# Three pairs of k-tiles by seven products instead of two in both output products of a streaming-encoder block

## The chip, the core and the metric

The kernel runs on one core of a Trainium2 chip. The metric is the device time of one execution in microseconds (us). TensorE (PE in the profile, with its weight loads as PEld), VectorE (DVE), ScalarE (ACT), GpSimd (POOL) and SyncE (SP, which issues the loads and stores here) each work through a queue of their own, in order, and wait for each other by semaphores.

## What is computed

One layer of an encoder block on 256 frames of width 2048, in float32. The residual stream `x` passes four parts, and the two whose last product changes stand in the middle:

```python
x = x + 0.5 * swiglu(rms_norm(x, ffn1_norm), ffn1_w_gate, ffn1_w_up, ffn1_w_down)
proj = rms_norm(x, mix_norm) @ w_in             # 2048 x 4112
x = x + concat([y_pool, y_gla]) @ w_out         # mixer's output product, 2048 x 2048
q = rms_norm(x, xattn_norm) @ w_q               # attention over 256 memory tokens
x = x + o @ w_o                                 # attention's output product, 2048 x 2048
x = x + 0.5 * swiglu(rms_norm(x, ffn2_norm), ffn2_w_gate, ffn2_w_up, ffn2_w_down)
return rms_norm(x, final_norm)
```

`y_pool` and `y_gla` (the pooling and the gated linear attention of the mixer) and `o` (four heads of 512) lie as the left operand `ys`; the activations of the other products lie as `xs`.

## The kernel before

**Precision.** TensorE multiplies in a reduced format (fp32r). Each operand is therefore split into a high part (a cast on ScalarE) and a remainder (a subtraction on VectorE), and each product is three on TensorE: high by high, high by remainder, remainder by high. The parts of a weight tile are called `wh` and `wl`, made at L1572 and L453.

**Units.** All weights are streamed. A unit is one load of 1 MB from `in_w...` into `raw` (L627, three buffers), the making of its parts, and its products. `Stream.emit` (L70) writes the making of unit u+2 in front of the products of unit u (`AHEAD` = 2), and a load three units ahead. From there a scheduler sets the order on each engine; `in_turn` and `among_weights` keep the makings, and what is put among them, in a fixed order on VectorE and ScalarE.

**The output products.** `into_x` (L821) runs two blocks of 1024 output columns. A block is eight units, one for each pair of k-tiles (256 rows of the weights), in the order that `orders` gives. A plain unit (L556) has 2 column halves x 2 row halves x 2 k-tiles x 3 = 24 products of 128x128 by 128x512 (L362). A unit whose pair is in `sevens` (L539) takes the 2x2x2 block product in a Strassen-Winograd form: 7 block products instead of 8, so 21 products (L507). It needs other operands: of the weights four sums `T` (three additions on VectorE, L486) and their parts (`wh` by L489, `wl` by L453) beside the parts of the three other weight blocks (`xh` by L279, `xl` by L280); of the activations sums that `Sums.make` (L413) forms once for each pair (L424 to L436, the splits at L285 and L286) and keeps in the tile `ye` and in `ys` itself. `OUTPUT` (L816) holds the pairs, the orders and the sums of both output products; `make_sums` (L810) says behind how many units each pair's sums are written.

**Joining and hand-over.** The partial sums of the sevens have four banks of their own. Behind the last seven of a block, `combine` (L570) joins them (L574 to L579) and `early_parts` (L765) adds them into `x` (L770). At the end of the block, two additions (L758) add the rest, `store_x` (L750) stores `x`, and `fold` (L785) turns it: 16 transposes (L791), eight splits on ScalarE (L248) and on VectorE (L240), and the squares for the norm (L800). Behind block 2 comes `finish_norm` (L299, L212 to L224). The next stage reads the folded `xs`: the attention's queries behind the mixer (L1366), the second feed-forward behind the attention.

**Homes.** In these stages `T`, `xh` and `xl` have no tiles of their own; `OUT_HOMES` (L1227) gives them in turn the tiles `kv`, `att` and `PT` of the attention.

Of the kernel before, what the change touches and what calls it, by code (L numbers as in the profile page):

```python
# [99 lines left out]
def build(ctx, tc, I, out):  # L100
# [90 lines left out]
    ys = main.tile([P, KT, 2, S], F32R, tag="ys", name="ys")  # L191
# [212 lines left out]
    class Sums:  # L404
# [4 lines left out]
        def __init__(self, name, act, pairs, over, room):  # L409
            self.name, self.act, self.pairs, self.over = name, act, pairs, over  # L410
            self.room, self.where = room, {}
# [390 lines left out]
    class IntoX:  # L802

        def __init__(self, pairs, after, orders, sevens, over=True):
            self.sums = Sums("ye", ys, pairs, over, 2)
            self.after, self.orders, self.sevens = after, orders, sevens

        def make_sums(self, after=None):  # L810
            for g, n in zip(self.sums.pairs, after or self.after):
# [1 line left out]

    WHOLE = IntoX((0, 4), (2, 5), ((1, 2, 3, 5, 0, 6, 4, 7), (1, 2, 0, 3, 4, 5, 6, 7)),
                  ((0, 4), (0, 4)))
    OUTPUT = IntoX((0, 4), (0, 4), ((1, 2, 3, 5, 0, 6, 4, 7), (1, 2, 0, 3, 4, 5, 6, 7)),  # L816
                   ((0, 4), (0, 4)))
    REST = IntoX((0,), (2,), ((1, 2, 3, 4, 0, 5), None), ((0,), ()), False)
    END = IntoX((0,), None, None, None)

    def into_x(w, act, scale, gain=None, k0=0, nk=KT, spread_too=True, src=None, way=OUTPUT):  # L821

        for b in range(2):
            st.op(lambda b=b: fetch_x(b, src), 2)
            cols = wwide(w, b * 2 * NB, k0, nk)
            if way.sevens[b]:
                block_s(cols, act, way.sums, way.orders[b], residual(scale, b, 0),
                        early_parts(scale, b), way.sevens[b])
            else:
                block_t(cols, act, residual(scale, b))  # L830
            if gain is not None:
                for j in range(2):
                    st.op(lambda c=2 * b + j: fold(c, gain), 1)
        if gain is not None:
            st.op(lambda: finish_norm(4, spread_too), 2)
            if spread_too:
                st.op(spread_norm, 3)
# [395 lines left out]
    def homes(of):  # L1233
        return lambda: scope.update(shared={tag: list(of[tag]) for tag in of})
# [35 lines left out]
                )  # L1270
        split_four(xs, 4 * c, v, G_MEM)

    OUTPUT.make_sums((1, 4))
    into_x(I["w_out"][0], ys, 1.0, G_X, spread_too=False)
    st.op(homes(Q_HOMES))
    st.op(mem_in, 2)
# [111 lines left out]
    st.op(homes(OUT_HOMES))  # L1388
    OUTPUT.make_sums()
    into_x(w_o, ys, 1.0, G_FFN2, spread_too=False)  # L1390
# [201 lines left out]
def program(shapes):  # L1592
    import concourse.bacc as _bacc

    nc = _bacc.Bacc("TRN2", target_bir_lowering=False, num_devices=1)
    args = {
        name: nc.dram_tensor(f"in_{name}", shapes[name], F32, kind="ExternalInput").ap()
        for name in _INS
    }
    out = nc.dram_tensor("out", _OUT, F32, kind="ExternalOutput").ap()  # L1600
    with tile.TileContext(nc, schedule_with_timeline_sim=True) as tc, ExitStack() as ctx:
        build(ctx, tc, args, out)
    return nc
# [10 lines left out]
```

## Time and profile before

| | |
|---|---|
| median of 3 runs | 2083.93 us (2083.45 to 2084.53) |
| profiled execution | 2082.87 us, span 2081.1 us, mean granted clock 0.999 |
| TensorE busy | 2069.4 us, 9660 recorded products |
| VectorE, ScalarE, GpSimd busy | 1786.8, 1138.7, 98.4 us |
| HBM read, written | 417.58 MB, 16.78 MB |

The page gives busy time by engine and then the chain of work that ended last, followed back from the last instruction. The costliest groups name the line, the engine, the tile written and the tiles read: `wl<-T,wh` at L453 is the remainder of a seven's sums, `wl<-raw,wh` the remainder of a plain tile. A timeline lists instructions by start and duration; a row with x2 holds two. Windows give the busy time of each engine between two times. All times count from the span's start.

### The profile page before, as it was taken

How to read it: one execution, taken by the hardware profiler on the slowest of the kernel's cores; microseconds unless marked ns; L12 is line 12 of the kernel's file. 1: busy time of each engine (PE TensorE's matmuls, PEld its weight loads, DVE VectorE, ACT ScalarE, POOL GpSimd, SP SyncE). 2: the span in 40 equal slices, each digit the busy share in tenths (PEclk: the TensorE clock that was granted, in tenths of full speed). 3: DMA queues.
4: the chain of work that ended last, by engine and by line, in shares of the span. 5: the costliest groups of instructions: out<-in, count | busy, mean ns of one | idle time of the engine just before them, and what ended most of it. 6: DMA issues, size and time to landing. Idle time of an engine off the chain costs nothing.

```text
span 2081.1 us, 24346 instructions
## 1 busy us (share of the span) xinstructions
PE 2069.4 (99%) x9660; PEld 1727.4 (83%) x9660; DVE 1786.8 (86%) x1670; ACT 1138.7 (55%) x1128; POOL 98.4 (5%) x87
## 2 busy tenths in 40 slices
PE   9999999999999999999999999999999999999998
PEld 7888888888888888888888888888888888888886
DVE  7998899989998677679788777879988999889987
ACT  7655455644654545455755444656554555545554
POOL 0000000000000000000000000000100010000001
PEclk9999999999999999999999999999999999999999
DMA  7666666566656755557655455666576665676664
GB/s 264 208 199 228 234 223 220 184 222 240 225 200 218 249 166 182 162 185 272 227 179 189 161 182 181 204 222 204 181 243 215 234 209 191 224 242 222 211 226 150
DMA packets 131322, 435.95 MB, mean 209 GB/s; under 512 B 9860, under 2 KB 13544, under 8 KB 130824
## 3 DMA queue, kind: packets, MB, share of 16 engines
q1 hardware_dynamic: 131176, 434.38, 61.8%
q8 instruction: 76, 1.25, 0.2%
q14 instruction: 38, 0.31, 0.0%
q10 hardware_dynamic: 32, 0.01, 0.0%
HBM read 417.58 MB, written 16.78 MB: 209 GB/s over the span
## 4 chain that ended last, share of the span: by engine, by line
PE 99%; DMA 0%; DVE 0%; ACT 0%; SPq 0%; DVEq 0%; issue 0%; ACTq 0%
PE pt L362 59%; PE pt L507 27%; PE pa L347 7%; PE pb L362 2%; PE ph L780 1%; PE pl L1319 1%; PE pv L1358 1%; PE px L791 1%; PE pp L1012 0%; PE pe L362 0%; DMA x<-in_x 0%; PE pa L1039 0%; PE po L1161 0%; PE tm L1267 0%; PE px L717 0%; PE pq L1148 0%
## 5 line engine op out<-in xcount | busy, mean ns | idle before, releaser
L362 PE MATMUL pt<-wh,xs 128*128 128x512 f32 x2128 | 682.4, 390 | 0.3 <-ACT xs L236 0.3
L453 DVE TENSOR_TENSOR wl<-raw,wh 128x2048 fp32r<-128x2048 f32 (+1 forms) x256 | 552.3, 2163 | 141.5 <-ACT wh L1572 141.1
L1572 ACT CAST wh<-raw 128x2048 fp32r<-128x2048 f32 x256 | 489.4, 1913 | 299.9 <-PE pt L362 138.4
L362 PEld LDWEIGHTS pt<-wh,xs 128*128 128x128 f32 x2128 | 398.7, 188 | 82.1 <-ACT xs L236 0.6
L362 PE MATMUL pt<-wh,ys 128*128 128x512 f32 x1472 | 463.8, 389 | 0.0
L489 ACT CAST wh<-T 128x1024 fp32r<-128x1024 f32 x236 | 248.1, 1055 | 363.8 <-DVE T L486 355.4
L362 PE MATMUL pt<-wl,xs 128*128 128x512 f32 x1064 | 414.6, 390 | 0.0
L362 PEld LDWEIGHTS pt<-wh,ys 128*128 128x128 f32 x1472 | 276.2, 188 | 56.9
L362 PE MATMUL pt<-wl,ys 128*128 128x512 f32 x736 | 286.8, 390 | 0.0
L453 DVE TENSOR_TENSOR wl<-T,wh 128x2048 fp32r<-128x2048 f32 (+1 forms) x118 | 264.8, 2244 | 0.8 <-ACT wh L489 0.4
L362 PEld LDWEIGHTS pt<-wl,xs 128*128 128x128 f32 x1064 | 199.8, 188 | 41.0 <-DVE wl L280 0.2
L280 DVE TENSOR_TENSOR xl<-raw,xh 128x1536 fp32r<-128x1536 f32 x118 | 206.7, 1752 | 18.9 <-ACT xh L279 18.9
L279 ACT CAST xh<-raw 128x1536 fp32r<-128x1536 f32 x118 | 174.6, 1479 | 45.1 <-PE pt L507 36.3
L486 DVE TENSOR_TENSOR T<-T,raw 128x512 f32<-128x512 f32 x236 | 163.0, 691 | 6.2
L362 PEld LDWEIGHTS pt<-wl,ys 128*128 128x128 f32 x736 | 138.2, 188 | 28.5
L486 DVE TENSOR_TENSOR T<-raw 128x1024 f32<-128x1024 f32 x118 | 143.9, 1220 | 0.5
L507 PE MATMUL pt<-wh,xs 128*128 128x512 f32 x364 | 141.8, 390 | 0.0
L457 POOL TENSOR_TENSOR wl<-raw,wh 128x768 fp32r<-128x768 f32 x40 | 74.0, 1851 | 1376.2 <-DVE wl L453 1351.4
L507 PE MATMUL pt<-xh,xs 128*128 128x512 f32 x364 | 135.8, 389 | 0.0
L347 PE MATMUL pa<-xs,wh 128*128 128x512 f32 x384 | 135.6, 397 | 0.0
L507 PE MATMUL pt<-wh,xe 128*128 128x512 f32 x320 | 124.3, 389 | 0.0
L347 PE MATMUL pa<-xs,wl 128*128 128x256 f32 x384 | 106.8, 282 | 0.0
(248 smaller groups left out, 2312.2 us busy)
## 6 DMA issues: line engine op xcount, KB each, us to landing
raw<-in_ffn_w_down SPq DMA_DIRECT2D x88, 1024.0 KB, 5.5
raw<-in_ffn_w_up SPq DMA_DIRECT2D x80, 1024.0 KB, 5.0
raw<-in_ffn_w_gate SPq DMA_DIRECT2D x77, 1024.0 KB, 5.1
raw<-in_w_in SPq DMA_DIRECT2D x32, 1024.0 KB, 5.2
raw<-in_xattn_w_kv SPq DMA_DIRECT2D x32, 1024.0 KB, 5.0
raw<-in_w_out SPq DMA_DIRECT2D x16, 1024.0 KB, 5.6
raw<-in_xattn_w_q SPq DMA_DIRECT2D x16, 1024.0 KB, 5.5
raw<-in_xattn_w_o SPq DMA_DIRECT2D x16, 1024.0 KB, 5.6
```

The lines of the kernel that those rows point to most:

```text
L279: in_turn("scalar", lambda: nc.scalar.copy(hi, src))
L280: in_turn("vector", lambda: nc.vector.tensor_tensor(out=lo, in0=src, in1=f32(hi), op=ALU.subtract))
L347: nc.tensor.matmul(o, w, x, start=k == 0 and i == 0, stop=last and i == 1)
L362: nc.tensor.matmul(ps, a, w, start=first and i == 0, stop=last and i == 2)
L453: in_turn("vector", lambda: nc.vector.tensor_tensor(out=lo[:, :n], in0=src[:, :n], in1=f32(hi[:, :n]), op=ALU.subtract))
L457: rest = nc.gpsimd.tensor_tensor(out=lo[:, n:], in0=src[:, n:], in1=f32(hi[:, n:]), op=ALU.subtract)
L486: in_turn("vector", lambda: nc.vector.tensor_tensor(out=o, in0=a, in1=b, op=ALU.add))
L489: in_turn("scalar", lambda: nc.scalar.copy(th[:, c], t[:, c]))
L507: nc.tensor.matmul(banks[n], x, w, start=n in fresh and j == 0, stop=n in ends and j == 2)
L780: nc.tensor.transpose(v[:, i, h * P : (h + 1) * P], g[:, h, i * P : (i + 1) * P], ident)
L791: nc.tensor.transpose(v[:, j, h * P : (h + 1) * P], x[:, h, j * P : (j + 1) * P], ident)
L1572: in_turn("scalar", lambda: nc.scalar.copy(hi, raw))
```

## The change

Both output products use `OUTPUT`. Before, pairs 0 and 4 went by seven in both blocks; block 1 took the units in the order 1 2 3 5 **0** 6 **4** 7 and block 2 in the order 1 2 **0** 3 **4** 5 6 7. Now pairs 2, 0 and 4 go by seven, block 1 in the order 1 3 5 6 **2 0 4** 7 and block 2 in the order 1 3 5 **2** 6 **0 4** 7. `ye` holds three pairs' sums instead of two. The sums of the mixer's pairs are written behind 1, 2 and 3 units (before: 1 and 4), those of the attention behind 0, 2 and 3 (before: 0 and 4).

```diff
-        def __init__(self, pairs, after, orders, sevens, over=True):
-            self.sums = Sums("ye", ys, pairs, over, 2)
+        def __init__(self, pairs, after, orders, sevens, over=True, room=2):
+            self.sums = Sums("ye", ys, pairs, over, room)
...
-    OUTPUT = IntoX((0, 4), (0, 4), ((1, 2, 3, 5, 0, 6, 4, 7), (1, 2, 0, 3, 4, 5, 6, 7)),
-                   ((0, 4), (0, 4)))
+    OUTPUT = IntoX((2, 0, 4), (0, 2, 3), ((1, 3, 5, 6, 2, 0, 4, 7), (1, 3, 5, 2, 6, 0, 4, 7)),
+                   ((2, 0, 4), (2, 0, 4)), room=3)
...
-    OUTPUT.make_sums((1, 4))
+    OUTPUT.make_sums((1, 2, 3))
```

The line numbers of the kernel stay the same.

## The prediction

> **What bounds the kernel now.** I read the page first: the busy line of each engine, then the chain that ended last.
>
> ```profile
> span 2081.1 us, 24346 instructions
> PE 2069.4 (99%) x9660; PEld 1727.4 (83%) x9660; DVE 1786.8 (86%) x1670; ACT 1138.7 (55%) x1128; POOL 98.4 (5%) x87
> ...
> PE 99%; DMA 0%; DVE 0%; ACT 0%; SPq 0%; DVEq 0%; issue 0%; ACTq 0%
> ```
>
> The chain is TensorE from end to end, so a product that is left out is worth its full time, as long as the operands of the next one are there. VectorE, at 86%, makes those operands. Its share differs by stage, so next I cut the two output products into windows: mixer block 1 and block 2, attention block 1 and block 2, each window with its hand-over.
>
> ```profile
> 912.00:953.00 41.00, 41.00 (x183) 33.92 (x182) 37.87 (x42) 25.75 (x24) 0.00 (x0) 1.00 0.68 227
> 953.00:1004.00 51.00, 51.00 (x236) 42.46 (x235) 44.15 (x40) 28.85 (x38) 0.00 (x0) 1.00 0.82 289
> 1296.00:1336.00 40.00, 40.00 (x191) 33.65 (x190) 33.38 (x33) 19.91 (x18) 0.00 (x0) 1.00 0.58 193
> 1336.00:1388.00 52.00, 52.00 (x248) 43.52 (x247) 43.25 (x47) 32.98 (x47) 0.00 (x0) 1.00 0.72 244
> ```
>
> The columns are length, then PE, PEld, DVE, ACT, POOL busy, the granted clock, the DMA share and GB/s. TensorE never rests and its clock is 1.00 in all four. VectorE has 3.1 us left in the first window, 6.9, 6.6 and 8.8 in the others.
>
> **The change part by part. (a) TensorE.** A plain pair of k-tiles is 24 products, one by seven is 21. Four more pairs go by seven (one in each block of both output products), so 12 products go; the built order of the changed kernel has exactly 12 fewer. The timeline of PE gives the step from one product to the next:
>
> ```profile
> 933.50 0.39 PE L507 MATMUL pt<-xh,ys 128*128 128x512 f32 x1
> ...
> 938.26 0.39 PE L507 MATMUL pt<-wh,ys 128*128 128x512 f32 x1
> ...
> 948.46 0.39 PE L507 MATMUL pt<-wh,ys 128*128 128x512 f32 x1
> ```
>
> 21 steps lie between the first two rows, 4.76 us: 0.227 us each (the 0.39 of a row overlaps the next). 12 x 0.227 = **2.7 us gained**.
>
> **(b) VectorE, more work.** The same stretch on VectorE's timeline holds the making of a pair by seven, a plain one, and the sums of one pair of k-tiles:
>
> ```profile
> 925.33 1.22 DVE L486 TENSOR_TENSOR T<-raw 128x1024 f32<-128x1024 f32 x1
> 926.47 0.55 DVE L286 TENSOR_TENSOR ye<-j,ye 128x384 fp32r<-128x384 f32 x1
> 926.93 1.41 DVE L486 TENSOR_TENSOR T<-T,raw 128x512 f32<-128x512 f32 x2
> 928.26 1.75 DVE L280 TENSOR_TENSOR xl<-raw,xh 128x1536 fp32r<-128x1536 f32 x1
> 929.93 2.28 DVE L453 TENSOR_TENSOR wl<-T,wh 128x2048 fp32r<-128x2048 f32 x1
> 932.13 2.29 DVE L453 TENSOR_TENSOR wl<-raw,wh 128x2048 fp32r<-128x2048 f32 x1
> 934.33 0.68 DVE L424 TENSOR_TENSOR j<-ys 128x512 f32<-128x512 f32 x1
> ...
> 936.45 1.22 DVE L486 TENSOR_TENSOR T<-raw 128x1024 f32<-128x1024 f32 x1
> ```
>
> From start to start: a pair by seven takes 925.33 to 932.13 less the 0.46 of the ye row, 6.34 us. A plain one takes 2.20 (932.13 to 934.33). The sums of a pair take 2.12 (934.33 to 936.45) and 0.46 for ye (926.47 to 926.93), 2.58 us. So each of the four exchanged pairs adds 4.14 us to VectorE, and the third pair's sums, made once for each output product, add 2.58: 4 x 4.14 + 2 x 2.58 = 21.7 us on VectorE against 2.7 us off TensorE. Where VectorE has no room, the difference becomes a wait of TensorE.
>
> **(c) Mixer, block 1.** In the changed order the three pairs by seven stand one behind the other, fifth to seventh of eight; before, a plain one stood between the two. A pair by seven lasts 4.77 us on TensorE (21 x 0.227) and 6.34 on VectorE, so three in a row eat the lead. In VectorE's new order from 925.33 stand: the ye row 0.46, the second pair's sums 2.58, the first making 6.34, the third pair's sums 2.58, the second making 6.34, then of the third T (925.33 to 926.47 and 926.93 to 928.26: 2.47) and xl 1.75. That is 22.5 us: the third xl is there at 947.9. In the new order of TensorE the first product that reads it is the 47th from the start of the first seven; it is due at 933.50 + 46 x 0.227 = 943.9. **Wait 3.9 us.** The window gives the same from the other side: 37.87 + 4.14 + 2.58 = 44.6 us of VectorE in 41.0 - 0.7 of TensorE, 4.3 over. I take 4.2. While a product waits, every later product waits with it; behind the waiting making of T the plain pairs' wl stand on VectorE, and nothing on ScalarE is needed sooner.
>
> **(d) The end of block 2, twice.** Before, the last pair by seven of block 2 is the fifth of eight, and its joining (L574 to L770) is over three plain pairs before the end. Now it is the seventh, as it is already in block 1. What stands behind it, in rows of block 1's end, of block 2's end, and of the first plain pairs of the stage behind:
>
> ```profile
> 961.05 1.22 DVE L758 SCALAR_TENSOR_TENSOR x<-pt,x 128x1024 f32<-128x1024 f32 x1
> ...
> 996.75 2.51 DVE L758 SCALAR_TENSOR_TENSOR x<-pt,x 128x1024 f32<-128x1024 f32 x2
> 999.98 2.29 DVE L453 TENSOR_TENSOR wl<-raw,wh 128x2048 fp32r<-128x2048 f32 x1 [0.72 <-ACT wh L1572]
> ...
> 1009.67 2.29 DVE L453 TENSOR_TENSOR wl<-raw,wh 128x2048 fp32r<-128x2048 f32 x1
> ```
>
> ```profile
> 997.83 0.39 PE L362 MATMUL pt<-wh,xs 128*128 128x512 f32 x1
> ...
> 1016.41 0.39 PE L362 MATMUL pt<-wl,xs 128*128 128x512 f32 x1
> ```
>
> Before, the last residual add (L758) of block 2 ends at 999.26, 1.4 us after TensorE began the next stage (997.83). Behind it run the squares, the norm, the eight splits (L240) and, in order behind those, the wl of the fourth pair of the queries, ready at 1011.96. Its first product is at 1016.41: 4.45 us to spare. In block 1, which ends as block 2 will now, the last add ends 13.6 us after the last product of the last pair by seven (948.46 + 0.23 to 962.27). 6.3 us of that is other work by the steps above (a wl 2.20, T 2.47 and xl 1.67 of the next making); in the new place two wl, 4.4, stand there: 11.7 to 13.6 us. Less the one plain pair behind it, 24 x 0.227 = 5.45, the last add ends 6.3 to 8.2 us into the next stage instead of 1.4: 4.9 to 6.8 later. Less the 4.45 to spare: a wait of 0.4 to 2.4 us. I take 2.0, near the upper end, because VectorE's wl also stands still for ScalarE at such an end (0.72 us at 999.98), which has its own half of the splits in front of its casts. The attention's end has the same shape, with the first plain pairs of ffn2 behind it:
>
> ```profile
> 1374.87 2.51 DVE L758 SCALAR_TENSOR_TENSOR x<-pt,x 128x1024 f32<-128x1024 f32 x2
> ...
> 1387.80 2.29 DVE L453 TENSOR_TENSOR wl<-raw,wh 128x2048 fp32r<-128x2048 f32 x1
> ```
>
> ```profile
> 1375.95 0.39 PE L362 MATMUL pt<-wh,xs 128*128 128x512 f32 x1
> ...
> 1394.49 0.39 PE L362 MATMUL pt<-wl,xs 128*128 128x512 f32 x1
> ```
>
> Spare there: 1394.49 - 1390.09 = 4.4 us; the same 2.0. **Together 4.0 us lost** (0.8 to 4.8).
>
> **(e) What costs nothing.** Attention block 1 has the same three in a row, but VectorE has 6.6 us idle in its window against 4.14 + 2.58 more and 0.7 less time: 0.8 over at worst. The first sums are due before the first unit there, so they move ahead of the window: 0, at most 0.8. Block 2 of both: 44.15 + 4.14 = 48.3 of 50.3, and 47.4 of 51.3; 0. ScalarE is at 26 of 41 in the tightest window; SP issues the same loads in another order, and its stores of x, which wait for L758, come some 6 us later with three raw buffers in front of them: 0, up to 1 if those run dry.
>
> [...]
>
> **Sum.** -2.7 + 4.2 + 4.0 = **+5.5 us**. On the profiled execution's own 2082.87 us (span 2081.1 and 1.8 around it) that is 2088.4; the median of the runs shown, 2083.93, is 1.06 above it, so the time to expect of a median is **2089.4 us**.
>
> **The rivals.** *VectorE's lead covers it (not slower).* The place is mixer block 1: if VectorE reached the first making some 4 us sooner (by 921 instead of 925.33), no product would wait, and with the spare of (d) just enough the 12 products alone remain: 2083.9 - 2.7 = 2081.2, within 0.2%. Against it: the window has 3.1 us idle in all, and the rows from 925.33 to 934.33 follow each other without a gap. *Throughput only.* Waits where VectorE's time overflows, (c) at 4.3 and (e) at 0.8, none at the ends: -2.7 + 5.1 = +2.4, 2086.3. For it: 4.4 us of spare; against it: 4.9 to 6.8 us of delay. *The waits feed on.* Both ends at 2.4, (e) at 0.8, 1 for late raw loads, block 1 at 4.4 : -2.7 + 4.4 + 4.8 + 0.8 + 1 = +8.3, 2092.2. For it: the DMA share of 0.82 around 953 to 1004; against it: the pairs behind the waits are plain, 5.45 us on TensorE to 2.20 on VectorE, so a backlog clears in two units.
>
> **How the numbers follow.** Forecast 0.62, lead covers 0.08, throughput only 0.14, waits feed on 0.16. The range takes the second and third rival and leaves the first and the far ends out: 2085.5 to 2093. About 0.2% (4.2 us) is what a measurement of this kernel can tell from no change; slower begins at 2088.1. Slower: 0.16 and most of the forecast's 0.62 = 0.74; the same: the first two rivals and the low side of the forecast, 0.24; faster needs more than the 2.7 us that go: 0.02.
>
> **What would show it.** In the changed kernel's waits, TensorE's L507 behind VectorE's xl (L280) and ScalarE's wh in mixer block 1, 4 us together; L362 behind wl (L453) about 10 us into the queries and into ffn2, 1 to 2.4 us each; none in attention block 1 or either block 2. PE busy goes down by 2.7 and its idle up by about 8. If the pairs by seven in block 1 follow each other without a gap, (c) is wrong; if the fourth plain pair of the next stage starts on time, (d) is wrong.

## The result, and the profile after

The changed kernel takes **2091.59 us** (median of 6 runs, 2089.93 to 2092.55) against 2083.86 us for the kernel before in the same comparison (6 runs, 2083.45 to 2084.53): ratio 1.0036, 95% interval [1.0025, 1.0047], **7.7 us slower**. The forecast was 2089.4 in 2085.5 to 2093.0.

The page of the changed kernel, the lines that answer to those of before:

```profile
span 2090.2 us, 24360 instructions
PE 2070.7 (99%) x9648; PEld 1725.9 (83%) x9648; DVE 1807.5 (86%) x1700; ACT 1146.6 (55%) x1140; POOL 98.4 (5%) x87
...
PE 97%; DVE 2%; ACT 1%; issue 0%; DMA 0%; SPq 0%; DVEq 0%; ACTq 0%
```

Twelve products fewer are recorded (9660 to 9648), VectorE is busy 20.7 us more, and the chain is no longer TensorE alone. TensorE still shows 99%: the shares of a whole kernel are too coarse for what happened, and the span less PE's busy time says it better: 11.7 us before (2081.1 - 2069.4), 19.5 after. The waits of TensorE name the places (line waited on, then us in total, times, longest):

```profile
PE pt L362 <- DVE wl L453: 3.2, 2, 1.6
PE pt L507 <- DVE xl L280: 3.1, 3, 1.9
...
PE pt L362 <- ACT wh L1572: 0.4, 1, 0.4
PE pt L507 <- ACT wh L489: 0.2, 1, 0.2
```

All four lines are new; L507 stands in mixer block 1 and L362 in the first plain pairs of the queries and of ffn2. The same four windows as in the prediction, in the changed kernel (the columns as there):

```profile
912.00:953.00 41.00, 37.80 (x163) 29.89 (x162) 38.40 (x50) 24.85 (x27) 0.00 (x0) 1.00 0.54 178
953.00:1004.00 51.00, 51.00 (x234) 42.45 (x233) 48.06 (x41) 28.58 (x34) 0.00 (x0) 1.00 0.79 285
1296.00:1336.00 40.00, 40.00 (x200) 34.09 (x199) 37.41 (x40) 22.14 (x23) 0.00 (x0) 1.00 0.48 155
1336.00:1388.00 52.00, 52.00 (x239) 43.28 (x238) 49.92 (x43) 28.14 (x32) 0.00 (x0) 1.00 0.73 248
```

TensorE rests in the first window alone. The other three, in which VectorE rose to 48.06, 37.41 and 49.92 us, stay full.

**Mixer block 1**, on PE's timeline (start, duration; in brackets the idle time before and its releaser):

```profile
938.98 0.61 PE L507 MATMUL pt<-xh,ys 128*128 128x512 f32 x2
939.80 0.50 PE L507 MATMUL pt<-wh,ye 128*128 128x512 f32 x1 [0.21 <-ACT wh L489]
942.18 0.50 PE L507 MATMUL pt<-xl,ys 128*128 128x512 f32 x1 [1.88 <-DVE xl L280]
...
947.24 0.39 PE L507 MATMUL pt<-wh,ye 128*128 128x512 f32 x1
948.64 0.50 PE L507 MATMUL pt<-xl,ys 128*128 128x512 f32 x1 [1.02 <-DVE xl L280]
```

A product should start 0.227 us behind the one before. 939.80 is due at 939.43 (0.37 late), 942.18 at 940.03 (2.16 late), 948.64 at 947.47 (1.18 late). One more is 0.26 late (944.38, behind the second seven's `wl`), and four steps behind such waits are 0.11 longer; together the block loses **4.40 us**. The bracket is less than the lateness because a product's row overlaps the next by 0.16, and that overlap is missing at a wait. VectorE beside it, where no row has an idle time in front from 926.40 to 955.11, the first row of the joining:

```profile
926.40 0.69 DVE L424 TENSOR_TENSOR j<-ys 128x512 f32<-128x512 f32 x1
...
946.84 1.75 DVE L280 TENSOR_TENSOR xl<-raw,xh 128x1536 fp32r<-128x1536 f32 x1
948.50 2.29 DVE L453 TENSOR_TENSOR wl<-T,wh 128x2048 fp32r<-128x2048 f32 x1
```

The third `xl` is ready at 948.59, and the product that reads it starts at 948.64.

**The two ends of block 2**, on VectorE: the mixer's last residual add and the two wl behind the splits, then the attention's last adds and the wl behind its splits.

```profile
1008.73 1.22 DVE L758 SCALAR_TENSOR_TENSOR x<-pt,x 128x1024 f32<-128x1024 f32 x1
...
1019.48 4.49 DVE L453 TENSOR_TENSOR wl<-raw,wh 128x2048 fp32r<-128x2048 f32 x2
...
1385.90 2.35 DVE L758 SCALAR_TENSOR_TENSOR x<-pt,x 128x1024 f32<-128x1024 f32 x2
...
1399.07 2.29 DVE L453 TENSOR_TENSOR wl<-raw,wh 128x2048 fp32r<-128x2048 f32 x1
```

On PE's timeline: the first product of the queries and its fourth pair's first `wl`, then the same of ffn2.

```profile
1001.51 0.39 PE L362 MATMUL pt<-wh,xs 128*128 128x512 f32 x1
...
1019.41 0.85 PE L362 MATMUL pt<-wh,xs 128*128 128x512 f32 x3
1021.82 0.50 PE L362 MATMUL pt<-wl,xs 128*128 128x512 f32 x1 [1.56 <-DVE wl L453]
...
1380.43 0.39 PE L362 MATMUL pt<-wh,xs 128*128 128x512 f32 x1
...
1399.09 0.74 PE L362 MATMUL pt<-wh,xs 128*128 128x512 f32 x2 [0.41 <-ACT wh L1572]
1401.42 0.79 PE L362 MATMUL pt<-wl,xs 128*128 128x512 f32 x1 [1.59 <-DVE wl L453]
1402.01 1.05 PE L362 MATMUL pt<-wh,xs 128*128 128x512 f32 x2
1402.86 0.63 PE L362 MATMUL pt<-wl,xs 128*128 128x512 f32 x1
```

The queries start at 1001.51, and the last add ends at 1009.95, 8.4 us into them; ffn2 starts at 1380.43, and the attention's last add ends at 1388.25, 7.8 us into it (before: 1.4). The fourth pair's `wl` comes late: 1.73 us lost in the queries (1019.41 + 3 x 0.227 = 1020.09, against 1021.82), 1.84 with the step behind it, and 2.45 in ffn2 (0.58 of it for a `wh` of ScalarE, at 1399.09). And the last two rows show what the prediction had not priced: behind the wait in ffn2 the products stand 0.43 us apart instead of 0.227 (1402.01, x2, to 1402.86). The window around it has the clock:

```profile
1400.00:1410.00 10.00, 8.58 (x31) 6.97 (x32) 9.73 (x15) 5.10 (x5) 0.00 (x0) 0.83 0.66 215
```

The seventh figure is the granted clock, 0.83: TensorE ran at half clock for 3.413 us by the trace's clock records, and seven steps in a row were 0.20 to 0.37 us too long, **1.56 us**.

Summed: -2.72 (12 products) + 4.40 (block 1) + 1.84 (queries) + 2.45 (ffn2) + 0.22 (a pair by seven in the queries, 0.85 of gaps against 0.63 before) + 1.56 (half clock) = +7.75. The medians differ by 7.73, but that they meet so closely is partly chance: the sum is read from one execution of each kernel, and these two differ by 9.16 (2092.03 and 2082.87). Of the other 1.4, 0.5 lies at the start, where TensorE waits 1.1 instead of 0.6 for the first load of `x`, and 0.6 behind the last product; 0.3 is not placed. Whether the other five executions of the changed kernel had the half clock, no trace shows.

### The profile page after: what moved, and what is told of

Read it like the earlier page. It is cut to its first block, busy times and chain, and to the rows that moved or that the text cites. A ratio compares the mean times of both kernels' runs of the same rounds, so it can differ in the third digit from the quotient of the medians.

```text
span 2090.2 us, 24360 instructions
## 1 busy us (share of the span) xinstructions
PE 2070.7 (99%) x9648; PEld 1725.9 (83%) x9648; DVE 1807.5 (86%) x1700; ACT 1146.6 (55%) x1140; POOL 98.4 (5%) x87
## 4 chain that ended last, share of the span: by engine, by line
PE 97%; DVE 2%; ACT 1%; issue 0%; DMA 0%; SPq 0%; DVEq 0%; ACTq 0%
PE pt L362 56%; PE pt L507 27%; PE pa L347 6%; PE pb L362 2%; PE ph L780 1%; DVE wl L453 1%; PE pl L1319 1%; PE pv L1358 1%; PE px L791 0%; DVE T L486 0%; PE pp L1012 0%; ACT xs L248 0%; DMA x<-in_x 0%; PE pe L362 0%; DVE xl L280 0%
## 5 line engine op out<-in xcount | busy, mean ns | idle before, releaser
L362 PE MATMUL pt<-wh,xs 128*128 128x512 f32 x2128 | 683.7, 391 | 0.5 <-ACT wh L1572 0.4
L453 DVE TENSOR_TENSOR wl<-raw,wh 128x2048 fp32r<-128x2048 f32 (+1 forms) x252 | 542.4, 2160 | 128.0 <-ACT wh L1572 127.7
L1572 ACT CAST wh<-raw 128x2048 fp32r<-128x2048 f32 x252 | 481.2, 1913 | 273.9 <-PE pt L362 118.7
L362 PEld LDWEIGHTS pt<-wh,xs 128*128 128x128 f32 x2128 | 399.2, 188 | 83.1 <-ACT wh L1572 1.0
L489 ACT CAST wh<-T 128x1024 fp32r<-128x1024 f32 x244 | 256.6, 1054 | 368.3 <-DVE T L486 355.1
L362 PE MATMUL pt<-wh,ys 128*128 128x512 f32 x1408 | 443.6, 389 | 0.0
L362 PE MATMUL pt<-wl,xs 128*128 128x512 f32 x1064 | 415.6, 391 | 3.2 <-DVE wl L453 3.2
L362 PEld LDWEIGHTS pt<-wh,ys 128*128 128x128 f32 x1408 | 264.2, 188 | 54.3
L453 DVE TENSOR_TENSOR wl<-T,wh 128x2048 fp32r<-128x2048 f32 (+1 forms) x122 | 273.9, 2245 | 1.3 <-ACT wh L489 0.9
L362 PE MATMUL pt<-wl,ys 128*128 128x512 f32 x704 | 274.5, 390 | 0.0
L362 PEld LDWEIGHTS pt<-wl,xs 128*128 128x128 f32 x1064 | 200.2, 188 | 45.0 <-DVE wl L453 4.0
L280 DVE TENSOR_TENSOR xl<-raw,xh 128x1536 fp32r<-128x1536 f32 x122 | 213.7, 1751 | 19.1 <-ACT xh L279 19.1
L279 ACT CAST xh<-raw 128x1536 fp32r<-128x1536 f32 x122 | 180.6, 1480 | 56.9 <-PE pt L507 39.7
L486 DVE TENSOR_TENSOR T<-T,raw 128x512 f32<-128x512 f32 x244 | 168.4, 690 | 6.5
L362 PEld LDWEIGHTS pt<-wl,ys 128*128 128x128 f32 x704 | 132.2, 188 | 27.3
L486 DVE TENSOR_TENSOR T<-raw 128x1024 f32<-128x1024 f32 x122 | 148.7, 1219 | 0.6
L507 PE MATMUL pt<-wh,xs 128*128 128x512 f32 x364 | 141.8, 390 | 0.0
L507 PE MATMUL pt<-xh,xs 128*128 128x512 f32 x364 | 135.8, 389 | 0.0
L507 PE MATMUL pt<-wh,xe 128*128 128x512 f32 x320 | 124.3, 389 | 0.0
```

Of the source, the lines that this page charges most:

```text
L279: in_turn("scalar", lambda: nc.scalar.copy(hi, src))
L280: in_turn("vector", lambda: nc.vector.tensor_tensor(out=lo, in0=src, in1=f32(hi), op=ALU.subtract))
L362: nc.tensor.matmul(ps, a, w, start=first and i == 0, stop=last and i == 2)
L453: in_turn("vector", lambda: nc.vector.tensor_tensor(out=lo[:, :n], in0=src[:, :n], in1=f32(hi[:, :n]), op=ALU.subtract))
L486: in_turn("vector", lambda: nc.vector.tensor_tensor(out=o, in0=a, in1=b, op=ALU.add))
L489: in_turn("scalar", lambda: nc.scalar.copy(th[:, c], t[:, c]))
```

## The experiments

The theory, **A**: each wait is VectorE's own queue at that place. In block 1 three makings stand one behind the other, at the ends of block 2 the joining stands in front of the next stage's remainders, and the half clock follows from the waits. Its rivals are stated with the runs they were put against. Beside e1 to e4 the kernel before has a median of 2083.41 (30 runs, 2082.65 to 2084.84), beside e5 to e8 a single time of 2084.24.

### One half of the change at a time

Rival **P**: the loss goes with the number of exchanged pairs, wherever they stand, so each output product gives half of it, 3.9 us. `e1_mixer_only` leaves the attention as it was before, `e2_attn_only` the mixer. In the diff, against the changed kernel, the first two additions are e1 (`MIXED` is the mixer's, `OUTPUT` the attention's); the last is the mixer's in e2, whose attention stays as changed.

```diff
+    MIXED = IntoX((2, 0, 4), (1, 2, 3), ((1, 3, 5, 6, 2, 0, 4, 7), (1, 3, 5, 2, 6, 0, 4, 7)),
+                  ((2, 0, 4), (2, 0, 4)), room=3)
+    OUTPUT = IntoX((0, 4), (0, 4), ((1, 2, 3, 5, 0, 6, 4, 7), (1, 2, 0, 3, 4, 5, 6, 7)),
+                   ((0, 4), (0, 4)), room=3)
...
+    MIXED = IntoX((0, 4), (1, 4), ((1, 2, 3, 5, 0, 6, 4, 7), (1, 2, 0, 3, 4, 5, 6, 7)),
+                  ((0, 4), (0, 4)), room=3)
```

> The mixer's output product as changed, the attention's as before. Theory A (VectorE's queue is late in two kinds of places: the third of three makings in a row in mixer block 1, and the fourth pair of the stage behind block 2): 6 products go (-1.4), block 1 waits as in the changed kernel (4.4), the queries' fourth pair waits (1.8), and 0.2 more in the queries: +5.1 us on before; the half clock of 3.4 us that the changed kernel's record shows at the start of ffn2 does not appear. Rival P (the two output products lose alike, since both have three pairs by seven late): about half of the changed kernel's +7.7, +3.9 us.

> The attention's output product as changed, the mixer's as before. Theory A: 6 products go (-1.4), no wait in attention block 1, 2.4 us of waits at the fourth pair of ffn2, and the half clock right behind them (1.6): +2.6 us; without the half clock +1.1. Together with the mixer's alone it gives the changed kernel's +7.7. Rival P: +3.9 us, with waits in attention block 1.

e1: 2089.09 (7 runs), ratio 1.0028 [1.0017, 1.0039], +5.7. e2: 2084.96 (10 runs, 2083.79 to 2086.04), ratio 1.0008 [0.9999, 1.0017], +1.6. The halves are not alike (the lowest time of e1 is 2088.50, the highest of e2 2086.04), and P falls; together they give 7.2 of the 7.7. Each half keeps the waits of its own places. TensorE's waits in e1, then in e2:

```profile
PE pt L507 <- DVE xl L280: 2.1, 2, 1.9
PE pt L362 <- DVE wl L453: 1.6, 1, 1.6
```

```profile
PE pt L362 <- DVE wl L453: 1.6, 1, 1.6
...
PE pt L362 <- ACT wh L1572: 0.4, 1, 0.4
```

One thing in e1 is not as expected. L507 waits twice and not three times, and the half clock is in block 1, right behind the long wait. Windows of e1:

```profile
935.00:945.00 10.00, 7.88 (x30) 5.85 (x29) 9.82 (x14) 3.84 (x5) 0.00 (x0) 0.90 0.43 136
945.00:955.00 10.00, 10.00 (x42) 7.86 (x41) 9.93 (x8) 7.90 (x7) 0.00 (x0) 0.93 0.60 186
```

The slow products give VectorE the time that the third making lacked (1.18 us of wait go, about 1.5 us of slow clock come), so block 1 costs about the same either way.

### Does the half clock belong to the waits?

The ten times of e2 fall in two groups of five, 2083.79 to 2084.47 (mean 2084.16) and 2085.44 to 2086.04 (mean 2085.67), 1.5 us apart. The profiled execution took 2086.04 and has the half clock. `e8_attn_again` is the same kernel once more.

> The kernel with the attention alone changed, run once more. Its 10 times lie in two groups, about 2084.2 and 2085.7 us. If the half clock behind the waits at the start of ffn2 depends on when the waits fall in the clock's own windows, a profile can have the same waits (0.6 and 1.8 us) without the record of half clock, and is then about 1.5 us shorter; if it belongs to the waits, every profile has it.

It took 2083.89. Its waits at ffn2 are those of e2; the window around ffn2's first pairs in e2, then in e8:

```profile
1390.00:1400.00 10.00, 8.01 (x28) 5.82 (x27) 9.50 (x16) 7.90 (x10) 0.00 (x0) 0.83 0.30 94
```

```profile
1390.00:1400.00 10.00, 8.02 (x34) 6.01 (x33) 9.88 (x17) 7.32 (x9) 0.00 (x0) 1.00 0.32 104
```

The same waits and PE busy time, but 28 products in the one and 34 in the other (e8 stands 0.58 us earlier there, which is two or three of the six). So the clock dropped behind these waits in one profiled execution of this kernel (0.83) and not in the other (1.00); 1.5 us, what the two groups lie apart, is its price, and it is not a fixed part of the change. That the five slower times of e2 are those with the half clock is likely, but only the profiled one shows it.

What differs may be where the waits fall. By the clock records of the changed kernel's trace, its stretches at full clock in front of the drop and behind it last 1396.051 and 679.252 us, 409 and 199 times 3.4133 (the one of before lasts 2071.890, 607 times), so the records of that trace lie on a grid of 3.413 us. The two waits on PE's timeline, in e2, then in e8:

```profile
1393.64 0.73 PE L362 MATMUL pt<-wh,xs 128*128 128x512 f32 x2 [0.39 <-ACT wh L1572]
1395.97 0.58 PE L362 MATMUL pt<-wl,xs 128*128 128x512 f32 x1 [1.59 <-DVE wl L453]
```

```profile
1393.06 0.73 PE L362 MATMUL pt<-wh,xs 128*128 128x512 f32 x2 [0.39 <-ACT wh L1572]
1395.39 0.50 PE L362 MATMUL pt<-wl,xs 128*128 128x512 f32 x1 [1.59 <-DVE wl L453]
```

In e2 the steps of the products are long from about 1396.3 on, and both waits lie in the 3.413 us in front of that: 2.3 us in which a product was due and had not started. Where the grid lies in e8, no view shows; that a boundary of it parts the two waits there is the author's estimate.

### Relieving VectorE at the ends

Rival **Q**: the ends wait for something other than VectorE's load, and relieving VectorE there changes nothing (+7.7). In `e3_share_ends` GpSimd makes 768 of the 2048 columns of `wl` for six units around the two ends, which the function offers already.

```diff
-        low_parts(tl, t, th, shared)
+        low_parts(tl, t, th, shared or u in (183, 184, 185, 247, 248, 249))
...
-                low_parts(lo, raw, hi, shared)
+                low_parts(lo, raw, hi, shared or u in (183, 184, 185, 247, 248, 249))
```

> The changed kernel, with 768 of 2048 columns of wl given to GpSimd for the second to fourth pair of the queries and of ffn2 (units 183 to 185 and 247 to 249). Before, such a part leaves VectorE 1.49 instead of 2.29 us, so some 0.8 us for each of three pairs, 2.4 us ahead of the fourth pair. Theory A: the waits at both ends go (1.8 and 2.4) and with them the half clock (1.6); block 1 keeps its 4.4: +7.7 - 5.8 = +1.9 us on before. Rival Q (the ends wait for ScalarE's splits of the fold and for the late store and loads, not for VectorE): the waits stay, +7.7 us.

2085.78 (10 runs, 2085.42 to 2085.99), ratio 1.0012 [1.0002, 1.0021], +2.4: 5.8 us below the changed kernel's median. Its waits:

```profile
PE pt L507 <- DVE xl L280: 3.1, 3, 1.9
```

Both L362 lines are gone, block 1's are the changed kernel's to a tenth, and the half clock is gone with the ends' waits (mean clock 0.999 over the span, in the changed kernel 0.998). Q falls. What is left, -2.72 + 4.40 + 0.22 = +1.9, is within 0.5 us of what was measured. The ends' own sum in the changed kernel is 1.84 + 2.45 + 1.56 = 5.85; 5.8 went by the medians themselves, 5.4 when each is taken against the kernel before beside it.

### Is block 1 a matter of the tiles' homes?

Rival **H**: in block 1 the makings are held up because the third `xh` must wait for a home, and not by VectorE's time. `e5_homes` swaps the order of the homes of `xh`.

```diff
-    OUT_HOMES = {"T": [("kv", D, 2)], "xh": [("kv", D, 2), ("att", 3 * NB, 2)],
+    OUT_HOMES = {"T": [("kv", D, 2)], "xh": [("att", 3 * NB, 2), ("kv", D, 2)],
```

> The changed kernel with the homes of xh in the other order: the first making of a row takes its xh from att and not from kv, so that the third making's xh no longer stands in the tile of the second's T. Theory A (VectorE's time): the waits in mixer block 1 stay at 4.4 us within 0.6. Rival H (the third making waits until an earlier one's tiles come free): they fall to 2 us or less. Of the ends neither says anything; they are read beside it.

2089.11, +4.9. Block 1 loses 4.4 us again, with the half clock in it as in e1 (two waits for `xl`, 2.0 us, where the changed kernel has three, 3.1); H falls. The swap did reach ScalarE, which starts the third `xh` at 940.77 instead of 944.41, but VectorE's third `xl` starts 20.55 us behind the first row of the second pair's sums (946.29 and 925.74), in the changed kernel 20.44 (946.84 and 926.40). That +4.9 is 2.8 us less than the changed kernel's +7.7, in one execution, has its larger part in the queries' wait (1.84), which is gone, since the mixer's last residual add now stands in front of a wl and not behind it. The wait of ffn2 stays (L362 for `wl`, once, 1.6 us), and here too the half clock stands behind it: the mean clock of the span is 0.997 (before 0.999), which fits two stretches of 3.4 us.

### Half of block 1's xl on GpSimd: a miss

With e5's homes, `e6_xl_shared` lets GpSimd make 768 of the 1536 columns of `xl` for the three units of block 1 (170 to 172).

```diff
+        at = 768 if u in (170, 171, 172) else 0
...
+                out=rl[:, at:], in0=raw[:, NB + at:], in1=f32(rh[:, at:]), op=ALU.subtract
...
+            nc.gpsimd.tensor_tensor(
+                out=rl[:, :at], in0=raw[:, NB : NB + at], in1=f32(rh[:, :at]), op=ALU.subtract
```

> The run before (homes in the other order), and for the three makings of mixer block 1 GpSimd makes half of xl (768 of 1536 columns), which takes 3 x 0.83 us off VectorE's row. Theory A: the third xl comes 2.5 us sooner, less what GpSimd's half (about 1.9 us) and ScalarE's casts now add: the waits in mixer block 1 fall from 4.4 to between 2 and 3.5 us. Rival H: no change against the run before.

2092.08, +7.8; block 1 lost 7.7 us (half clock included; mean clock of the span 0.998, before 0.999) where waits of 2 to 3.5 were expected. VectorE's rows in that kernel, then GpSimd's:

```profile
928.04 1.81 DVE L286 TENSOR_TENSOR ys<-j,ys 128x128 fp32r<-128x128 f32 x1
...
940.00 2.20 DVE L486 TENSOR_TENSOR T<-T,raw 128x512 f32<-128x512 f32 x1
...
946.60 2.87 DVE L486 TENSOR_TENSOR T<-raw 128x1024 f32<-128x1024 f32 x1
...
950.83 0.95 DVE L490 TENSOR_TENSOR xl<-raw,xh 128x768 fp32r<-128x768 f32 x1
```

```profile
927.74 1.96 POOL L494 TENSOR_TENSOR xl<-raw,xh 128x768 fp32r<-128x768 f32 x1 [131.47 <-ACT xh L488]
939.44 2.21 POOL L494 TENSOR_TENSOR xl<-raw,xh 128x768 fp32r<-128x768 f32 x1 [9.73 <-ACT xh L488]
945.80 2.57 POOL L494 TENSOR_TENSOR xl<-raw,xh 128x768 fp32r<-128x768 f32 x1 [4.15 <-ACT xh L488]
```

Each of the first three VectorE rows begins while a GpSimd row runs and ends 0.15, 0.55 and 1.10 us behind it, a little less than it takes alone: 1.81 instead of 0.29 us, 2.20 instead of 0.69, 2.87 instead of 1.22. That is 4.7 us lost for three halves of an `xl`, each of which saves 0.8. The third `xl` is ready at 951.78 instead of 948.59, 3.2 us later, and block 1's loss is 3.3 us larger. The edit made things worse, yet it moved VectorE and the loss of TensorE by nearly the same amount, as A has it.

### The pairs by seven early in block 2

Rival **L**: only a pair by seven *late* in block 2 costs anything, so in block 2's old order the ends are free and block 1's loss alone remains (+1.9). `e7_block2_early` keeps three pairs in both blocks and gives block 2 its old order.

```diff
-    OUTPUT = IntoX((2, 0, 4), (0, 2, 3), ((1, 3, 5, 6, 2, 0, 4, 7), (1, 3, 5, 2, 6, 0, 4, 7)),
+    OUTPUT = IntoX((2, 0, 4), (0, 2, 3), ((1, 3, 5, 6, 2, 0, 4, 7), (1, 2, 0, 3, 4, 5, 6, 7)),
```

> The changed kernel with block 2's order 1 2 0 3 4 5 6 7 in both output products: three pairs by seven as now, but as second, third and fifth unit, so that the joining is over three plain pairs before the end. Rival L (what costs at the ends is the late place alone): the waits of 1.8 and 2.4 us and the half clock go, nothing comes: +7.7 - 5.8 = +1.9 us on before. Theory A (VectorE's queue, wherever it is full): they go too, but two makings in a row (12.7 us) now stand in front of block 1's joining, last adds and fold, of 7.6 us and more, while TensorE has some 15 us of products there: new waits of 4 to 8 us in block 2 of each output product, +10 to +18 us in all.

2098.22, **+14.0**: L falls. The waits at the ends are gone, and larger ones stand behind the seam of block 1 and block 2, in the mixer and in the attention:

```profile
PE px L791 <- DVE x L758: 5.8, 2, 2.9
PE pt L507 <- DVE xl L280: 2.9, 2, 1.9
...
PE pt L362 <- DVE wl L453: 1.0, 1, 1.0
```

The transposes of block 1's result (L791) wait 2.9 us in each of the two output products for the residual adds. Ten microseconds around the mixer's (from 965) show VectorE full and the clock at 0.66:

```profile
965.00:975.00 10.00, 6.60 (x26) 5.36 (x25) 10.00 (x9) 7.29 (x12) 0.00 (x0) 0.66 0.76 255
```

VectorE has the end of three pairs by seven, their joining and the next pairs by seven in one stretch. The trace has two stretches of half clock: 6.8 us here (0.66 over 10 us), and 3.4 in the attention, where the clock is 0.95 over the ten microseconds from 1345 and the products' steps are long up to 1357. Late in block 2 is the better place; it only needs spare behind it.

### Where there is room, and nowhere else

`e4_best` takes the third pair where VectorE has time for it: mixer block 1 stays at two pairs, the other three blocks have three, and the ends are shared as in e3. `MIXED` is the mixer's, and the attention's `OUTPUT` stays as changed. Nine products go.

```diff
+    MIXED = IntoX((0, 4, 2), (1, 4, 6), ((1, 2, 3, 5, 0, 6, 4, 7), (1, 3, 5, 2, 6, 0, 4, 7)),
+                  ((0, 4), (2, 0, 4)), room=3)
```

> Mixer: pairs 0 and 4 by seven in block 1 in the order of before, pairs 2, 0 and 4 in block 2 in the changed order; attention as changed; the wl of the second to fourth pair behind both ends shared with GpSimd as in the run before. 9 products go. Theory A: no three makings in a row in mixer block 1, ends relieved: no wait that before doesn't have, -9 x 0.227 = -2.0 us on before, at least -1.5. Rival Q: the ends still wait, 4 to 6 us: +2 to +4 us.

2082.36 (11 runs, 2081.41 to 2083.35), ratio 0.9994 [0.9985, 1.0002]: 1.1 us faster, less than the least that was expected, in an interval that holds no change. Its only wait in these stages:

```profile
PE pt L507 <- DVE xl L280: 0.2, 1, 0.2
```

Against the changed kernel it is better by far (the intervals do not meet); that it beats the kernel before is not shown. The profiled execution took 2081.41, 1.46 below the profiled one of before (2082.87): nine products are 2.04, and longer gaps in the queries (0.91 against 0.63) and two steps of 0.11 in ffn2 take 0.5 back. The times of e4 lie in a group of five (2081.41 to 2081.60) and six that are 0.8 to 1.9 above it; what adds this, in the kernel before too (2082.65 to 2084.84), stays open.

## Why the prediction was right, and where it was short

The direction, the range and the places of the waits came out as forecast; the size was 2.2 us short (+5.5 against +7.7).

- **(a) TensorE, -2.7.** Right: 12 recorded products fewer at 0.227 us. No run shows the gain alone; e4, with nine products fewer, is 1.46 shorter between the profiled executions and has 0.5 of small gaps more.
- **(b) VectorE, +21.7.** Right: +20.7 by the page. Start-to-start steps, as the prediction took them, count the little time between rows and the busy figure doesn't, which may be part of the 1.0 between them.
- **(c) Mixer block 1, 4.2.** Right in cause and size: 4.40. The third `xl` was forecast for 947.9; the first seven of the block started 0.49 later than before (933.99), and `xl` was ready at 948.59. The prediction reckoned the whole wait at the third `xl`; in the trace 2.5 us of it come at the second seven already (its `wh` and `xl`) and 1.2 at the third. e5 takes the homes away as a cause, and e6 moves the making by 3.2 and the loss by 3.3.
- **(d) The two ends, 2.0 each.** Right in cause, slightly small: 1.84 and 2.45, together 4.29. The last add was forecast 6.3 to 8.2 us into the next stage and came 8.4 and 7.8 us into it. Taking the upper end was right; its reason, ScalarE's casts, shows in ffn2 as 0.41 us of a wait for `wh` by the bracket. e3 removes both.
- **(e) No waits in attention block 1 and in either block 2.** Right: PE is full in the three windows, and no load of weights appears in TensorE's waits.
- **The step that failed is the sum.** It held that a wait costs its own length. In ffn2 the half clock behind the wait cost 1.56 more, and in the queries 0.22 came on top. The clock was 1.00 in all four windows of before (0.999 over the span), so no row there could show this price; a place with waits of about 2 us close together (2.45 lost in ffn2 itself) should have had a chance of it in its term. In mixer block 1 the same execution had a wait of 2.16 and kept its clock, and the other executions of the changed kernel may differ. The range reached 2093 for other reasons.
- **"PE busy goes down by 2.7"** did not show: it went up by 1.3. Products behind a wait and at half clock have longer rows (0.50 and 0.63 us instead of 0.39), and a wait takes away the overlap of two rows. "Its idle up by about 8" did: 19.5 - 11.7 = 7.8.
- **The rivals.** "Lead covers" lacks all the waits that stand in the trace; "throughput only" had block 1 (4.3) and lacks the ends. "The waits feed on" gave 2092.2, closer to the measured time than the forecast's 2089.4, but by terms that did not occur: no 0.8 in attention block 1 and no late loads. What fed on was the clock.
- **Busy time alone does not decide.** The change loads VectorE 20.7 us more and lost; e4 loads it 14.5 us more than before (1801.3 against 1786.8) and is not slower. Where the work stands in the queue decides.

## What to carry to other kernels

Price a saving on the busiest engine also in the queue of the engine that feeds it, stage by stage and in that queue's order: here 2.7 us saved cost 8.7 us of waits with VectorE at 86% before and after. Work that is moved to the end of a stage needs its spare in the first tiles of the next stage; look for the first of them that stands behind the hand-over. Give a clock drop its chance where a forecast makes TensorE wait as here: behind the same 2.3 us of waits it came in one of two profiled executions of one kernel, and cost about 1.5 us.

## What the runs showed of the hardware

**The clock behind short waits.** In e2's profiled execution TensorE went to half clock (0.83 over 10 us) behind waits of 0.55 and 1.76 us (0.57 us of work between them, by the starts of the products), 2.3 us in all; in e8 the same waits left it at 1.00. The half clock lasts 3.413 us in the changed kernel's clock records and twice that, 6.8, in one of e7's two stretches. On the grid of 3.413 us that the records of the changed kernel give, the drop at 1401.14 stands behind a stretch with 2.17 us in which a product was due and had not started. No other stretch up to there has over 1.95; that is mixer block 1, where a boundary at 940.34 cuts the long wait, and it has no drop. In e1 the same two waits of mixer block 1 (0.39 and 2.16 us late, from 939.07 to 941.85) had the half clock behind them from about 943.0 (0.90 and 0.93 in its two windows). That the place of the waits on such a grid decides is the author's estimate from these executions; no run moved a wait to test it.

**VectorE beside GpSimd.** In e6 each of three VectorE rows (L286 and twice L486) that began beside a GpSimd subtraction did not end before that one had, but 0.15 to 1.10 us behind it, roughly as if it had begun only then: 0.29 us became 1.81, 0.69 became 2.20, 1.22 became 2.87. What holds them up, no run shows. e3 paid the same toll, on VectorE and beside it on GpSimd:

```profile
1019.03 3.83 DVE L453 TENSOR_TENSOR wl<-raw,wh 128x2048 fp32r<-128x2048 f32 x1 [0.31 <-ACT wh L1572]
```

```profile
1018.86 1.85 POOL L457 TENSOR_TENSOR wl<-raw,wh 128x768 fp32r<-128x768 f32 x1 [7.59 <-issue]
```

That VectorE row takes 2.29 us elsewhere and here ends 2.15 us behind GpSimd's; what sharing gained at the ends (0.8 us for each `wl`, 1.49 instead of 2.29, and an earlier place in the queue) was still enough for the waits there.
